# Order of loads and reuse of tiles in a one-core trunk of two gated linear-attention branches

## The chip, the cores and the metric

The kernel runs on one core of a Trainium2 chip. It uses five engines, which are called here as the profile names them: PE (TensorE, the matmuls, with PEld for its weight loads), DVE (VectorE), ACT (ScalarE), POOL (GpSimd) and SP (SyncE). Each engine works through its own instructions in order; DMA transfers are issued from the queue of one of them. The metric is the device time in microseconds (us) of the core, as the median of the runs. The kernel before took 1220.32 us (three runs, 1220.21 to 1222.69).

## The reference

The computation is one layer of a decoder trunk, batch 1, 1024 positions, width 1024, everything in float32:

```python
mod = silu(c) @ ada_w + ada_b
shift, scale, gate = split(mod, 3)
h = rms_norm(x, norm_w) * (1 + scale) + shift
hq, hf, hi, hz, gq, gk, gv, gz, ga, mg = split(h @ w_in)      # widths 4 x 1024, 2 x 512, 2 x 1024, 16, 2048
y_h = hgrn2_branch(hq, hf, hi, hz, lb, hgrn_norm_w)           # 8 heads of 128
y_g = gla_branch(gq, gk, gv, gz, ga, alpha_w, alpha_b, gla_norm_w)   # 4 heads, keys of 128, values of 256
u_h, u_g = y_h @ w_branch[0], y_g @ w_branch[1]
merged = sigmoid(mg[0]) * u_h + sigmoid(mg[1]) * u_g
out = rms_norm(x + gate * (merged @ w_out), final_norm_w)
```

Each branch is a causal gated recurrence, `S_t = diag(a_t) S_{t-1} + k_t v_t^T`, `o_t = S_t^T q_t`, computed in chunks of 64 positions, then normalised and multiplied by a SiLU gate.

## The kernel before

**Storage.** SBUF holds 46 slots of 128 x 1024 floats. `Slots.get` takes the slot that has been free longest (the free list is a plain queue), and names the tile by a serial number (`b_8146`), so that a high number is a late tile. `Halves` lends out halves of a slot. A new tile in a slot can be written only once every reader of the slot's last tile is done. Where that reader is a store to DRAM, the new tile's load or cast waits for the store.

**Products in three matmuls.** A float32 operand is parted into a high part, which ACT makes by a cast, and a low part, which DVE makes by a subtraction: `split` (cast L196, subtraction L197) in the first stages, `prep_duo` (L1333, L1334) and `build`, for the other operand (L1311, L1312, or L1308 with a sign, for one product of the seven), in the last. Each product is high by high, high by low, and low by high.

**First stages, to about 800 us.** `Stream` goes through jobs of the combined projection (matmuls L541, L352 and others), loading the weights of two jobs ahead and parting one ahead. Between its matmuls it weaves in two tracks, each a generator that yields a number of units of PE work after which it wants to go on:

- the side track: the projection's outputs through SiLU (for one, L952 and L953 read PE's bank), and the chunked attention (L657 to L850). Its solve of a block goes to and fro between engines: DVE L676 to L679, PE L683, DVE L687 to L710 with the masked copies L698, PE L715, and so on to DVE L785 and ACT L790 to L796;
- the back track, here called background: `prepare`, `gate_side` (eight rows of `ada_w` summed into the output gate) and `out_weights`. `prepare` forms differences of the activations, and by `weight_sums` (L1188 to L1209, additions around L1200) the sums of weight blocks that a Winograd form needs, and stores them to `ws`. `out_weights` loads `w_out` (`load_wy`), multiplies it by the gate (`gate_wy`, L1233), adds (`sum_wy`, L1242), and stores to `wo` from L1228.

**Last stages, from about 800 us.** Four blocks (two halves of `mg`, two branch projections) are each computed by seven products in a Winograd form. Each product takes two duos of weight tiles: 56 duos, each used by 24 matmuls at L1391. A duo is loaded by `load_duo` (L1322 whole from `ws`, or two halves by L1326 from `w_in` or `w_branch`), and parted by `prep_duo`. `ahead(n, loads, preps)` stands in front of duo n's matmuls and sees to it that all duos below n + loads have their load issued and all below n + preps are parted. `scale_quad` (L1290) multiplies the other operand by its normalisation for the last block. The results pass through ACT's copies (L1363, L1365, L1371) and DVE's sums (L1378); for the first block `put_gate1` takes a sigmoid (L1462) and stores it from POOL (L1463, `gate`), for the third DVE multiplies (L1477). Products by `w_out` and the final norm follow from L1537 on.

**What sets the order.** The program is emitted in the order of the code, with yields deciding where the tracks come in. The framework then puts each engine's instructions in order by its own estimates and by the dependencies, and adds the waits. So a change of the numbers in a yield, of the arguments of `ahead`, or of the slot that `get` returns may change the order on any engine. Loads are issued from SP, stores from POOL; within each queue they go in order.

Of the kernel before, what the change touches and what calls it, by code (L numbers as in the profile page):

```python
# [34 lines left out]
class Slots:  # L35


    def __init__(self, pool, n):
        self.pool = pool
        self.free_list = deque(range(n))  # L40
        self.owner = {}
        self.serial = 0

    def get(self, shape, dtype=F32):
        i = self.free_list.popleft()
        self.serial += 1
        t = self.pool.tile([P] + list(shape), dtype, tag=f"s{i}", name=f"b{self.serial}")
        self.owner[id(t)] = (i, t)
        return t

    def free(self, *tiles):
        for t in tiles:
            self.free_list.append(self.owner.pop(id(t))[0])


class Halves:
# [5 lines left out]
    def get(self):  # L62
        if not self.open:
            t = self.slots.get([2, 512])
            left = [0, t]
# [6 lines left out]
    def free(self, *views):  # L72
        for v in views:
            v, left = self.owner.pop(id(v))
            left[0] -= 1
            if left[0]:
                self.open.append((v, left))
            else:
                self.open = deque(z for z in self.open if z[1] is not left)
                self.slots.free(left[1])  # L80
# [3 lines left out]
def hybrid_trunk_kernel(  # L84
# [6 lines left out]
    nc = tc.nc  # L91
# [952 lines left out]
    def gate_side():  # L1044
# [3 lines left out]
        for k in range(KT):  # L1048
# [7 lines left out]
            yield 1  # L1056
# [102 lines left out]
    def factors(acts, f):  # L1159
        sub = nc.vector.tensor_sub  # L1160
        for kk in range(2):
# [7 lines left out]
            for p, dst, a, b in ((5, "11", "12", "11"), (7, "12", "12", "22"), (6, "22", "22", "11"), (4, "21", "21", "22")):  # L1169
                sub(y[dst], y[a], y[b])  # L1170
                nc.gpsimd.dma_start(f[p][kk], y[dst])
                if p == 7:
                    S.free(y["12"])
                elif p == 6:
                    S.free(y["11"])
                yield 1.5
            S.free(y["22"], y["21"])
# [10 lines left out]
    def weight_sums(b, i):  # L1188
# [19 lines left out]
        S.free(x1, x2, s1, s2)  # L1208
# [36 lines left out]
    def out_weights():  # L1245
        for kk in range(2):
            while len(S.free_list) < 12:
                yield 1
            load_wy(kk)
            yield 8  # L1250
# [7 lines left out]
            S.free(*wy.values())  # L1258
# [201 lines left out]
    def put_gate1(d, half, ap, summed):  # L1460
# [3 lines left out]
        Q.free(g)  # L1464
# [222 lines left out]
    def begin_2():  # L1687
        build(GROUPS[0])
        fetch_factor(GROUPS[1])
        ahead(0, 4, 1)  # L1690
# [38 lines left out]
```

## Time and profile before

| | kernel before |
|---|---|
| median of three runs | 1220.32 us |
| the profiled execution | 1226.09 us |
| span in its trace | 1224.2 us |
| granted TensorE clock, mean | 0.993 |
| busy PE / PEld | 1186.9 / 987.0 us |
| busy DVE / ACT / POOL | 793.4 / 548.5 / 124.4 us |
| read from HBM / written | 132.87 / 49.28 MB |
| mean transfer rate | 149 GB/s |

The span runs from the first to the last instruction in the trace; the execution's own time has a little around it. PE and PEld overlap. A row of the timeline gives a start, a duration, the engine, the line, output and inputs without their numbers, and in brackets the time that the engine was idle ahead of it and what ended the idle time. Line numbers in rows are those of the kernel that the row comes from.

### The profile page before, as it was taken

What the parts mean: (1) busy time and instruction counts of PE and PEld (TensorE: products, weight loads), DVE (VectorE), ACT (ScalarE), POOL (GpSimd) and SP (SyncE); (2) the same over time, 40 slices, a digit from 0 to 9 for tenths busy, and PEclk for the clock granted to TensorE, in tenths of its full rate; (3) what the DMA queues carried; (4) which work ended last, traced back from release to release, by engine and by line L of the source; (5) the groups of instructions that cost most, each with busy time, mean ns of one, the idle gap of its engine ahead of it and who ended that gap; (6) DMA issues with size and microseconds to landing.
All of it is one profiled execution on the core that took longest, in us unless ns stands there. A gap on an engine that the chain in (4) does not pass through costs nothing.

```text
span 1224.2 us, 20849 instructions
## 1 busy us (share of the span) xinstructions
PE 1186.9 (97%) x8575; PEld 987.0 (81%) x8575; DVE 793.4 (65%) x1247; ACT 548.5 (45%) x798; POOL 124.4 (10%) x215
## 2 busy tenths in 40 slices
PE   5999999999999999999999989999999999999997
PEld 3777889899898888888888878877778888878886
DVE  4636444774938465877787575694532666988994
ACT  5646722434344243424433324445733544544554
POOL 4100000202112122022011201011010000000000
PEclk9999999999999999999999999989999999999999
DMA  9714000845453267265165522144465646435523
GB/s 321 271 69 138 18 19 20 291 139 182 146 173 122 82 214 233 93 198 175 60 241 190 193 101 87 35 157 159 135 206 167 196 137 211 150 103 172 165 104 128
DMA packets 130960, 183.51 MB, mean 150 GB/s; under 512 B 7467, under 2 KB 97633, under 8 KB 130866
## 3 DMA queue, kind: packets, MB, share of 16 engines
q1 hardware_dynamic: 117250, 136.87, 36.1%
q0 software_dynamic: 13568, 45.31, 9.6%
q8 instruction: 67, 1.10, 0.4%
q14 instruction: 27, 0.22, 0.1%
q10 hardware_dynamic: 48, 0.01, 0.0%
HBM read 132.87 MB, written 49.28 MB: 149 GB/s over the span
## 4 chain that ended last, share of the span: by engine, by line
PE 59%; issue 22%; DMA 4%; ACT 3%; DVE 3%; POOL 2%; SPq 0%; POOLq 0%; ACTq 0%; DVEq 0%
PE pd L541 16%; PE pd L1391 10%; PE sc_ps L1391 5%; PE pm L1391 5%; PE pd L1537 3%; PE pd L643 2%; PE pd L644 2%; PE pd L645 2%; DMA b<-in_w_in_dram 2%; PE sc_ps L1537 2%; PE pm L848 1%; PE pm L829 1%; PE pm L850 1%; PE pd L352 1%; PE pm L1537 1%
## 5 line engine op out<-in xcount | busy, mean ns | idle before, releaser
L541 PE MATMUL pd<-b,b 128*128 128x512 f32 x1632 | 388.9, 395 | 0.0
L541 PEld LDWEIGHTS pd<-b,b 128*128 128x128 f32 x1632 | 303.3, 188 | 65.6 <-issue 1.7
L1391 PE MATMUL pd<-b,b 128*128 128x512 f32 x720 | 177.6, 399 | 8.6 <-ACT b L1462 3.0
L1391 PEld LDWEIGHTS pd<-b,b 128*128 128x128 f32 x720 | 136.9, 192 | 40.9 <-ACT b L1462 4.0
L197 DVE TENSOR_TENSOR b<-b,b 128x1024 fp32r<-128x1024 f32 (+2 forms) x90 | 99.2, 1114 | 79.0 <-ACT b L196 66.2
L196 ACT CAST b<-b 128x1024 fp32r<-128x1024 f32 (+2 forms) x90 | 84.0, 949 | 111.0 <-PE pd L541 19.9
L1334 DVE TENSOR_TENSOR b<-b,b 128x1024 fp32r<-128x1024 f32 x56 | 69.8, 1249 | 72.8 <-ACT b L1333 43.0
L1333 ACT CAST b<-b 128x1024 fp32r<-128x1024 f32 x56 | 58.3, 1048 | 65.2 <-PE pd L1391 18.9
L1391 PE MATMUL sc_ps<-b,b 128*128 128x512 f32 x324 | 79.4, 391 | 1.0 <-ACT scT L793 1.0
L600 PE MATMUL pd<-b,b 128*128 128x256 f32 x256 | 74.2, 290 | 0.0
L602 PE MATMUL pd<-b,b 128*128 128x256 f32 x256 | 72.5, 283 | 0.0
L601 PE MATMUL pd<-b,b 128*128 128x256 f32 x256 | 72.4, 283 | 0.0
L1391 PE MATMUL pm<-b,b 128*128 128x512 f32 x300 | 72.2, 389 | 0.0
L1391 PEld LDWEIGHTS sc_ps<-b,b 128*128 128x128 f32 x324 | 60.3, 188 | 14.3 <-ACT scT L793 1.4
L1312 DVE TENSOR_TENSOR b<-b,b 128x1024 fp32r<-128x1024 f32 x48 | 57.7, 1223 | 19.7 <-ACT b L1311 12.5
L1311 ACT CAST b<-b 128x1024 fp32r<-128x1024 f32 x48 | 49.7, 1048 | 44.7 <-PE pd L1391 15.8
L1391 PEld LDWEIGHTS pm<-b,b 128*128 128x128 f32 x300 | 56.5, 188 | 11.8
L352 PE MATMUL pd<-b,b 128*128 128x512 f32 x192 | 53.2, 410 | 1.6 <-ACT b L196 0.9
L1206 POOL DMA_DIRECT2D ws<-b x64 | 34.6, 541 | 192.0 <-DVE b L1200 86.5
L735 ACT COPY xb<-b 128x512 f32<-128x512 f32 x48 | 29.3, 620 | 52.5 <-PE sc_ps L715 23.6
L643 PE MATMUL pd<-b,b 128*128 128x512 f32 x128 | 51.2, 400 | 0.0
L644 PE MATMUL pd<-b,b 128*128 128x512 f32 x128 | 50.0, 390 | 0.0
(286 smaller groups left out, 1965.4 us busy)
## 6 DMA issues: line engine op xcount, KB each, us to landing
b<-in_w_in_dram SPq DMA_DIRECT2D x66, 512.0 KB, 4.4
ws<-b POOLq DMA_DIRECT2D x64, 256.0 KB, 3.2
b<-ws SPq DMA_DIRECT2D x32, 512.0 KB, 3.8
b<-in_x_dram SPq DMA_DIRECT2D x16, 512.0 KB, 6.0
b<-in_ada_w_dram SPq DMA_DIRECT2D x32, 256.0 KB, 6.7
b<-in_w_branch_dram SPq DMA_DIRECT2D x16, 512.0 KB, 4.5
b<-h SPq DMA_DIRECT2D x14, 512.0 KB, 4.6
wo<-b POOLq DMA_DIRECT2D x14, 512.0 KB, 3.8
```

Source lines behind the costliest of these rows:

```text
L196: nc.scalar.copy(hi, src)
L197: nc.vector.tensor_sub(lo, src, hi.bitcast(F32))
L352: nc.tensor.matmul(accs[f], wg(a, d, f), b[d][:, half * 512:half * 512 + 512], start=(d == 0 and n == 0), stop=(d == KT - 1 and n == 2))
L541: nc.tensor.matmul(ps[0:w, th * 512:(th + 1) * 512], a[:, k, 0:w], b[:, th * 512:(th + 1) * 512], start=(k == 0 and n == 0), stop=(k == KT ...
L600: nc.tensor.matmul(o, lh, hi[:, k % 4, :], start=(k == 0), stop=False)
L601: nc.tensor.matmul(o, lh, lo[:, k % 4, :], start=False, stop=False)
L602: nc.tensor.matmul(o, ll, hi[:, k % 4, :], start=False, stop=(k == KT - 1))
L643: nc.tensor.matmul(o, lh, hi[:, k % 2, :], start=(k == 0), stop=False)
L644: nc.tensor.matmul(o, lh, lo[:, k % 2, :], start=False, stop=False)
L1334: nc.vector.tensor_sub(lo, t, hi.bitcast(F32))
L1391: nc.tensor.matmul(o, a[:, sl], c, start=(p in (1, 5) and kt == 0 and n == 0), stop=(kt == 3 and n == 2), skip_group_check=True)
L1537: nc.tensor.matmul(o, a, b, start=(p in (1, 5) and kt == 0 and n == 0), stop=(kt == 3 and n == 2), skip_group_check=True)
```

## The change

Three things change; no computation is added or taken away.

**The free list** becomes a heap. A freed slot gets as its key the serial number of the latest tile taken so far, and `get` returns the lowest key. A slot that is freed behind a store (`sent=True`: the activations in `put_act`, the differences and sums in `prepare`, the `w_out` tiles, the gate halves in `put_gate1`) gets a key that is eight higher, as if it had been freed eight tiles later.

**The background.** `gate_side` yields 1.5 units after each row in place of 1. `load_wy` loads one tile in a call, and `out_weights` yields 2 units after each of the four and 2 more behind them, where before all four loads stood together, with 8 units behind them.

**The last stages.** `ahead` is called with 5 and 1 in place of 4 and 2 (in `begin_2`, ahead of the first duo, 5 and 1 in place of 4 and 1): a duo's load is issued one duo earlier, and its cast and subtraction come one duo later.

```diff
 class Slots:
-        self.free_list = deque(range(n))
+        self.free_list = [(-1, i - n, i) for i in range(n)]
+        self.freed = 0
 ...
     def get(self, shape, dtype=F32):
-        i = self.free_list.popleft()
+        i = heapq.heappop(self.free_list)[-1]
 ...
-    def free(self, *tiles):
+    def free(self, *tiles, sent=False):
         for t in tiles:
-            self.free_list.append(self.owner.pop(id(t))[0])
+            self.freed += 1
+            heapq.heappush(self.free_list, (self.serial + (8 if sent else 0), self.freed, self.owner.pop(id(t))[0]))
 ...
     # Halves.free
+            left[2] |= sent
             if left[0]:
                 self.open.append((v, left))
             else:
                 self.open = deque(z for z in self.open if z[1] is not left)
-                self.slots.free(left[1])
+                self.slots.free(left[1], sent=left[2])
 ...
     def put_act(acts, d, y):
-        S.free(y)
+        S.free(y, sent=True)
 ...
     # gate_side, after each row
             S.free(b)
-            yield 1
+            yield 1.5
 ...
     # factors (and so the two frees ahead of it)
-            S.free(y["22"], y["21"])
+            S.free(y["22"], y["21"], sent=True)
 ...
     # weight_sums
-        S.free(x1, x2, s1, s2)
+        S.free(x1, x2)
+        S.free(s1, s2, sent=True)
 ...
-    def load_wy(kk):
-        for kh in range(2):
-            for f in range(2):
-                t = wy[kh, f] = S.get([2, 512])
-                nc.sync.dma_start(t, w_rows[kh][:, 2 * kk:2 * kk + 2, f * 512:f * 512 + 512])
+    def load_wy(kk, n):
+        kh, f = n // 2, n % 2
+        t = wy[kh, f] = S.get([2, 512])
+        nc.sync.dma_start(t, w_rows[kh][:, 2 * kk:2 * kk + 2, f * 512:f * 512 + 512])
 ...
     # out_weights
-            load_wy(kk)
-            yield 8
+            for n in range(4):
+                load_wy(kk, n)
+                yield 2
+            yield 2
 ...
-            S.free(*wy.values())
+            S.free(*wy.values(), sent=True)
 ...
     # last_stages
-                    ahead(2 * n + i // 2, 4, 2)
+                    ahead(2 * n + i // 2, 5, 1)
 ...
     # put_gate1
-        Q.free(g)
+        Q.free(g, sent=True)
 ...
     # begin_2
-        ahead(0, 4, 1)
+        ahead(0, 5, 1)
```

The changed file has four lines more ahead of `out_weights` and six more ahead of the last stages: L197 there is L201, L679 is L683, L698 is L702, L1233 is L1237, L1242 is L1246, L1334 is L1340, L1462 is L1468.

At three places the rows of an engine are shown, first of the kernel before and then of the changed one. The first is DVE at the solve of an attention block, some 710 us into the span of the kernel before. `xb` is the solve's operand, on which PE's matmul L683 (L687 in the changed kernel) waits; the rows on 128x1024 tiles are subtractions of weights and products of the background.

```order
769 L676 TENSOR_TENSOR xb<-b_6490,b_6552 128x32x8
770 L677 TENSOR_TENSOR xb<-b_6490,b_6552 128x32x8x2
771 L685 TENSOR_TENSOR b_6490<-b_6490,b_6552 128x256
772 L678 TENSOR_TENSOR xb<-xb,b_6552 128x32x16
773 L197 TENSOR_TENSOR b_7015<-b_6864,b_7014 128x1024
774 L679 TENSOR_TENSOR xb<-xb,b_6552 128x32x8
775 L687 TENSOR_TENSOR b_6552<-b_6552 128x256
```

The same place of DVE in the changed kernel:

```order
768 L682 TENSOR_TENSOR xb<-xb,b_6550 128x32x16
769 L1237 TENSOR_TENSOR b_6871<-b_6871,b_6058 128x1024
770 L683 TENSOR_TENSOR xb<-xb,b_6550 128x32x8
771 L691 TENSOR_TENSOR b_6550<-b_6550 128x256
772 L690 TENSOR_TENSOR b_6488<-xb,b_6550 128x256x3
773 L692 TENSOR_TENSOR b_6550<-b_6550 128x256
774 L201 TENSOR_TENSOR b_7015<-b_6862,b_7014 128x1024
775 L705 TENSOR_TENSOR tot_726<-b_6550 128x256
776 L1246 TENSOR_TENSOR b_6767<-b_6767,b_6871 128x1024
777 L694 TENSOR_TENSOR blk<-sc_ps,eye_679 128x256
```

The weight subtraction has moved from ahead of the last `xb` row to four rows behind it, and two background rows on `w_out` tiles (L1237 and L1246) have come in, one ahead of that row.

The second is ACT in the first of the last stages, some 900 us into the span. The casts L1333 (L1339) make the high parts of duos; the L1462 (L1468) on `pd` frees the bank for which PE's next matmuls wait.

```order
492 L1333 CAST b_8261<-b_8191 128x1024
493 L1462 ACTIVATE b_7872<-b_7872 128x512
494 L1462 ACTIVATE b_7938<-b_7938 128x512
495 L1333 CAST b_8331<-b_8265 128x1024
496 L1333 CAST b_8298<-b_8228 128x1024
497 L1462 ACTIVATE b_7938<-b_7938 128x512
498 L1462 ACTIVATE b_8243<-pd_7492 128x512
```

The same place of ACT in the changed kernel:

```order
493 L1468 ACTIVATE b_7870<-b_7870 128x512
494 L1468 ACTIVATE b_7936<-b_7936 128x512
495 L1339 CAST b_8297<-b_8145 128x1024
496 L1468 ACTIVATE b_7936<-b_7936 128x512
497 L1339 CAST b_8394<-b_8264 128x1024
498 L1468 ACTIVATE b_8242<-pd_7494 128x512
499 L1339 CAST b_8361<-b_8227 128x1024
```

Of the two casts that stood together ahead of the last two sigmoids, b_8298 (now b_8297) stands one sigmoid earlier, and b_8331 is no longer there: in front of the sigmoid on `pd` stands the cast of another tile (b_8394), and the loads' tiles have lower numbers.

The third is DVE at about 1035 us, where it makes the low parts of duos for PE's next products.

```order
1014 L1290 TENSOR_TENSOR b_9157<-b_9157,b_7956 128x1024
1015 L1378 TENSOR_TENSOR b_9129<-b_9129,sc_ps 128x512
1016 L1290 TENSOR_TENSOR b_9158<-b_9158,b_7956 128x1024
1017 L1477 TENSOR_TENSOR b_8751<-b_8751,b_9129 128x512
1018 L1334 TENSOR_TENSOR b_9162<-b_9081,b_9161 128x1024
```

The same place of DVE in the changed kernel:

```order
1014 L1296 TENSOR_TENSOR b_9156<-b_9156,b_7954 128x1024
1015 L1384 TENSOR_TENSOR b_9128<-b_9128,sc_ps 128x512
1016 L1296 TENSOR_TENSOR b_9157<-b_9157,b_7954 128x1024
1017 L1483 TENSOR_TENSOR b_8750<-b_8750,b_9128 128x512
1018 L1340 TENSOR_TENSOR b_9161<-b_9002,b_9160 128x1024
```

The rows stand in the same order, but the subtraction in the last of them reads another load (b_9002 in place of b_9081): it belongs to the duo one before.

More of the change, by code (lines that the diff above doesn't have):

```diff
@@ L1 @@
+import heapq
 from collections import deque
@@ L64, in get @@
             t = self.slots.get([2, 512])
-            left = [0, t]
+            left = [0, t, False]
             self.open.extend((t[:, i, :], left) for i in range(2))
@@ L70, in get, with free @@
         return v
-    def free(self, *views):
+    def free(self, *views, sent=False):
         for v in views:
@@ L1172, in factors @@
                 if p == 7:
-                    S.free(y["12"])
+                    S.free(y["12"], sent=True)
                 elif p == 6:
-                    S.free(y["11"])
+                    S.free(y["11"], sent=True)
                 yield 1.5
-            S.free(y["22"], y["21"])
+            S.free(y["22"], y["21"], sent=True)
     def branch(n, d):
```

## The prediction

> **What bounds the kernel now.** I read, in this order, the page's busy times, the busy time by stretches of the span, the TensorE timeline where a stretch loses time, and the chain that ended last. Line numbers are those of the kernel before.
>
> ```profile
> PE 1186.9 (97%) x8575; PEld 987.0 (81%) x8575; DVE 793.4 (65%) x1247; ACT 548.5 (45%) x798; POOL 124.4 (10%) x215
> ```
>
> TensorE (PE) is busy 97% of the span, so only what makes PE wait, or run slowly, counts. By stretches (span, then busy us of PE, PEld, DVE, ACT, POOL, then granted clock, DMA share, GB/s):
>
> ```profile
> 700.00:750.00 50.00, 46.85 (x438) 38.50 (x437) 31.70 (x59) 16.89 (x27) 1.59 (x3) 0.97 0.30 95
> 800.00:850.00 50.00, 45.66 (x422) 36.23 (x421) 34.14 (x59) 25.27 (x41) 5.22 (x6) 0.93 0.46 155
> 850.00:900.00 50.00, 46.45 (x212) 37.65 (x210) 24.92 (x24) 32.00 (x40) 7.22 (x10) 1.00 0.56 176
> 900.00:950.00 50.00, 48.76 (x208) 40.17 (x209) 12.17 (x10) 18.58 (x27) 2.69 (x5) 0.97 0.55 176
> 1032.00:1080.00 48.00, 48.00 (x212) 39.35 (x211) 46.14 (x51) 21.83 (x25) 0.00 (x0) 1.00 0.50 152
> ```
>
> The first four lose 3.15, 4.34, 3.55 and 1.24 us. The last loses nothing on PE, but there DVE is busy 46.14 of 48. The PE timeline shows where the loss sits (start, us, what, and in brackets the wait before it and its releaser):
>
> ```profile
> 717.35 1.76 PE L683 MATMUL sc_ps<-xb,b 128*32 128x80 f32 x64 [3.15 <-DVE xb L679]
> 719.04 6.89 PE L541 MATMUL pd<-b,b 128*128 128x512 f32 x24
> 725.85 0.89 PE L715 MATMUL sc_ps<-xb,b 128*32 128x48 f32 x64
> ...
> 814.59 8.49 PE L1391 MATMUL pd<-b,b 128*128 128x512 f32 x24 [2.96 <-DVE b L953]
> 823.01 0.89 PE L715 MATMUL sc_ps<-xb,b 128*32 128x48 f32 x64
> ...
> 839.49 1.88 PE L1391 MATMUL sc_ps<-b,b 128*128 128x512 f32 x7 [0.97 <-ACT scT L793]
> 841.66 1.19 PE L1391 MATMUL pd<-b,b 128*128 128x512 f32 x4 [0.29 <-ACT b L1462]
> ...
> 857.92 3.02 PE L1391 MATMUL pd<-b,b 128*128 128x512 f32 x12 [1.17 <-ACT b L1363]
> ...
> 887.38 3.02 PE L1391 MATMUL pd<-b,b 128*128 128x512 f32 x12 [0.94 <-DVE b L1378]
> ...
> 894.77 2.88 PE L1391 MATMUL pd<-b,b 128*128 128x512 f32 x12
> 897.49 1.07 PE L1391 MATMUL pm<-b,b 128*128 128x512 f32 x4
> 901.24 4.58 PE L1391 MATMUL pd<-b,b 128*128 128x512 f32 x12 [2.68 <-ACT b L1462]
> 905.62 4.80 PE L1391 MATMUL pm<-b,b 128*128 128x512 f32 x20
> ...
> 1087.93 1.21 PE L1391 MATMUL pd<-b,b 128*128 128x512 f32 x4 [0.44 <-DVE b L1483]
> ```
>
> I call the three large ones A (717), B (814) and C (901). Start to start, 12 matmuls take 2.72 us from 894.77 to 897.49, so 24 take 5.44. After A they take 6.81 (719.04 to 725.85), after B 8.42 (814.59 to 823.01), and after C 12 take 4.38 (901.24 to 905.62): PE runs slowly behind each large wait, for 1.37, 2.98 and 1.66 us more. Waits (12.60) and slowness (6.01) are 18.6 us together, 1.5% of the time: the most that better ordered loads could give.
>
> The Trainium skill, page "TensorE: Matmul & The Clock Gate", section "Part 1: The HAM clock gate", says that the clock halves after at least one idle window of some 3.4 us. Here it fell behind waits of 2.68 and 2.96 us, so the trace disagrees on the bound. By the Trainium skill a shorter wait costs itself alone; what that would make of the sum is a rival below.
>
> The chain names what was late:
>
> ```profile
> 702.54 3.27 DMA wo<-b
> 706.30 7.96 DMA b<-in_w_in_dram
> ...
> 886.29 3.86 DMA gate<-b
> 891.79 6.30 DMA b<-in_w_in_dram
> ```
>
> Ahead of A and of C stands the same pair: a store (wo, gate), and then a load into the tile or through the queue that the store held up. This is what the change works on.
>
> **The change, place by place.** The heap and the yields run while the program is built and cost the chip nothing. No load, store, cast or subtraction is added or taken away; all are moved, in the order of each engine and of SP's queue. So each term is a wait that goes or comes. The profiled execution took 1226.09 us (span 1224.2 and 1.89 around it), 5.77 above the median of 1220.32; I work out waits in it and take their sum from the median.
>
> A. DVE works in order, and L679, which PE awaits, stands behind a weight subtraction L197:
>
> ```profile
> 711.01 0.88 DVE L678 TENSOR_TENSOR xb<-xb,b 128x512 f32<-128x512 f32 x1
> 715.43 1.23 DVE L197 TENSOR_TENSOR b<-b,b 128x1024 fp32r<-128x1024 f32 x1 [3.53 <-ACT b L196]
> 716.57 0.63 DVE L679 TENSOR_TENSOR xb<-xb,b 128x256 f32<-128x256 f32 x1
> ...
> 723.77 0.43 DVE L698 COPY_PREDICATED blk<-mask,sc_ps 128x64 f32<-128x64 int32 x1
> ```
>
> In the changed order L197 stands four rows later, and ahead of L679 comes a gate product L1233, whose load goes out beside the same w_in load at about 706 (both tiles are freed by PE's L541). Nothing shows how long that load takes there: between the page's median for such loads (4.4, below) and the 7.96 above it lands at 710.4 to 714.0. With 1.23 for L1233 and 0.63 for L679, behind L678's end at 711.9, L679 ends between 713.8 and 715.9; PE is free at 714.2 (717.35 less 3.15). I take no wait, since two wo stores that run at that time before are now queued later; 1.7 is the other end. But from L679 to L698 DVE now carries L197 and one L1242 more (1.2 each) and one L717 (0.9) less: 7.6 us (716.57 to 724.20) become 9.1. From 713.2 that ends at 722.3, and PE reaches L715 at 714.2+1.7+5.44 = 721.3. What is late next is L698, by 1.0. A gives 3.15+1.37-1.0 = 3.5; its ends are 0.5 and 4.5.
>
> ```profile
> b<-in_w_in_dram SPq DMA_DIRECT2D x66, 512.0 KB, 4.4
> ```
>
> B. ScalarE (ACT) holds the release of PE's bank (L952, then DVE's L953) behind a cast whose target waits for a store:
>
> ```profile
> 808.83 2.00 ACT L1311 CAST b<-b 128x1024 fp32r<-128x1024 f32 x2 [4.23 <-DMA yh<-b]
> 810.73 1.06 ACT L1308 ACTIVATE b<-b 128x1024 fp32r<-128x1024 f32 x1
> 811.69 1.00 ACT L952 ACTIVATE b<-pd 128x1024 f32<-128x1024 f32 x1
> ```
>
> The changed order still has a cast that waits for this yh store (an L1333 now): all other tiles are in use, so ranking the tile later only names another user. L1308 moves behind L952, but three DVE subtractions stay ahead of L953. B gives 0.4, between -0.5 (the store 0.9 later) and 1.0 (the L1308).
>
> 838 to 842. L1308 (1.06) no longer stands ahead of the sigmoid L1462, and one cast has left ACT's row there; DVE's last step of the block solve (L785) follows some 0.6 sooner. Of 0.97 and 0.29 I take 0.9; ends 0 and 1.3. At 887 the subtraction L1334 moves behind L1378, for which PE waits 0.94: 0.8, ends 0 and 0.94. 857 stays: it hangs on GpSimd's L1110, which does not move.
>
> C. SP issues in order, and its queue is held by the gate stores:
>
> ```profile
> 879.81 12.48 SPq L1326 DMA_DIRECT2D b<-in_w_in_dram  x8
> ...
> 898.18 1.99 ACT L1333 CAST b<-b 128x1024 fp32r<-128x1024 f32 x2 [4.58 <-DMA b<-in_w_in_dram]
> 900.08 0.62 ACT L1462 ACTIVATE b<-b 128x512 f32<-128x512 f32 x1
> 900.61 0.58 ACT L1462 ACTIVATE b<-pd 128x512 f32<-128x512 f32 x1
> ```
>
> Eight half loads take from 879.81 to 892.3; the last pair lands at 898.1 (891.79 + 6.30); two casts wait for it and PE's L1462 stands behind them. With tiles behind gate stores ranked later, three of these four duos wait for matmuls or subtractions that end between 861 and 866, and go out then, some 14 to 25 us sooner. Of ACT's two casts one moves behind the L1462 and the other waits only for PE at 894. The L1462 comes at 896.8+0.6+0.6 = 898.0 (PE itself 0.9 earlier), where PE is free at 897.7. C gives 2.68+1.66, less 0.3: 4.0; ends 1.0 (the wait halves, the clock still falls) and 4.3. At 1087 an L1334 leaves DVE ahead of L1483: 0.4, ends 0 and 0.44.
>
> New waits. Parting one duo later takes 5.44 us, one step's matmuls, from every duo's lead. Compared with their first use, most leads stay above 3 us. In the stretch with DVE busy 96% one does not:
>
> ```profile
> 1036.15 1.23 DVE L1334 TENSOR_TENSOR b<-b,b 128x1024 fp32r<-128x1024 f32 x1
> ```
>
> The L1334 at 1036.15 belonged to the duo that PE takes at 1041.3; in that place now stands the duo that PE needs at 1036.3. It ends at 1037.4: a wait of 1.1. It gives the following duos 1.1 more, and with DVE's durations laid end to end they then come 0.4 to 2 us in time. The unseen cost reaches from 0.5 to a whole step, 5.4. At 824 an L1308 now stands ahead of PE's L1365: 0.4, ends 0 and 1. At 497 an L1200 that waits for a load and a store stands where L197 stood ahead of L679:
>
> ```profile
> 495.01 1.22 DVE L197 TENSOR_TENSOR b<-b,b 128x1024 fp32r<-128x1024 f32 x1
> 496.14 0.63 DVE L679 TENSOR_TENSOR xb<-xb,b 128x256 f32<-128x256 f32 x1
> 497.35 1.31 PE L683 MATMUL sc_ps<-xb,b 128*32 128x80 f32 x64
> ```
>
> Its load can go out at about 490.7, when the last reader of its tile ends, so by 4.4 to 7.96 it lands at 495.1 to 498.7; L1200 and L679 add 1.3: 0 to 2.6 late, and I take 0.5. The gate rows and the w_out loads, spread over more steps, end well before their L1233; I cost that at nothing, covered by 4 us or more of PE work ahead of their use.
>
> Sum: 3.5+0.4+0.9+0.8+4.0+0.4 = 10.0 gained, 1.1+0.4+0.5 = 2.0 lost, so 8.0, and 1212.3. The profiled run is slow by 5.77 for reasons unseen; if part of its stalls is missing in timed runs, so is part of the gain, and I forecast 1213.
>
> **Rivals.** *A background load holds DVE in order* (slower). For it: the load before A took 7.96, not 4.4, and the changed order has such a row directly ahead of L679 at 497, 542 and 714. Against: by the issues worked out above only the slow price makes them late. Each such wait costs what A cost, 3.15+1.37 = 4.5. If 714 waits as before, its 3.5 is gone; with 4.5 at 497 and 542 too, against 0.5, the sum is 8.0-3.5-8.5 = -4.0: 1224.3. It decides from the third such place on; with two it is no change. The Trainium skill, "DMA: Bandwidth & Descriptors", section "Issuing engines are not separate DMA queues", says that loads and stores of all issuers share 16 engines; the 7.96 beside wo stores agrees, and speaks against loads that go out earlier in a bunch.
>
> *Half the gain*: one of A and C keeps its wait since the next late item is as late (a wo store for L1242, a gate store for the other cast). For it: B, where the changed order keeps the store. 8.0 less 3.5 or 4.0: about 1216.
>
> *Slow PE has another cause* and stays behind A and C: 8.0-1.37-1.66 = 5.0, 1215.3. Against it: 24 matmuls are slow behind A, B and C only. (The Trainium skill's 3.4 us would leave the same.)
>
> *Nothing moves that counts*: tiles are so scarce that the heap returns the same waits, as at B: 1220. Against: at C the predecessors differ.
>
> *B goes too*: 2.96+2.98 more, 1207.
>
> **How the numbers follow.** Forecast 0.44 (1209 to 1215); half the gain 0.15; slow PE 0.05; B too 0.03: faster together 0.67. Nothing 0.08. Slower 0.25. A measurement of this kernel tells some 0.2% (2.4 us) from no change. The range from 1207 to 1224.5 takes in the slower case at its price and leaves out the part of it that costs more.
>
> **What would show it.** Right: no PE wait over 0.5 at L683 near 714, one near 1 at L715; none over 0.5 at L1462 near 898, and its 12 matmuls in 2.72; B as before; one of about 1 near 1028 at L1391, released by L1334. Wrong: waits at L683 near 497 or 542 released by L679; PE waiting for L1334 in step after step from 1030 to 1080; w_in loads over 6 us at C.

## The result, and the profile after

The changed kernel takes 1232.61 us (median of five runs, 1230.35 to 1233.43) against 1221.18 us for the kernel before (five runs). The ratio is 1.0087, with a 95% interval from 1.0070 to 1.0104: it is slower, and lies outside the range that was forecast. The profiled execution took 1233.43 us (span 1231.7).

The page of the changed kernel gives nearly the same busy times as before, in 7.5 us more of span:

```profile
PE 1188.9 (97%) x8575; PEld 986.9 (80%) x8575; DVE 795.5 (65%) x1247; ACT 548.2 (45%) x798; POOL 122.7 (10%) x215
```

The busy time of the changed kernel by stretches (columns as in the prediction):

```profile
200.00:250.00 50.00, 45.64 (x396) 40.86 (x396) 26.32 (x38) 15.90 (x19) 8.01 (x12) 0.96 0.60 214
350.00:400.00 50.00, 46.16 (x399) 41.15 (x398) 29.59 (x53) 21.63 (x26) 9.39 (x14) 0.97 0.53 174
710.00:760.00 50.00, 49.29 (x455) 40.65 (x454) 35.87 (x63) 16.14 (x27) 3.20 (x6) 1.00 0.33 117
800.00:850.00 50.00, 45.92 (x432) 36.77 (x431) 40.25 (x65) 26.33 (x40) 4.52 (x5) 0.97 0.46 156
850.00:900.00 50.00, 48.54 (x233) 39.88 (x233) 25.52 (x29) 33.22 (x45) 7.23 (x10) 1.00 0.59 186
900.00:950.00 50.00, 50.00 (x221) 41.13 (x221) 13.99 (x13) 21.22 (x29) 3.79 (x7) 1.00 0.57 190
```

The stretches of A and C, from 700 to 750 and from 850 to 950, have mostly recovered, and 800 to 850 (B) has not, as forecast. But two stretches in which PE was busy for 50.00 of 50 us before, from 200 to 250 and from 350 to 400, now lose 4.36 and 3.84 us, with a lower granted clock. The timeline of PE in the changed kernel shows what they are, and what became of A, B and the place at 1036:

```profile
235.73 7.09 PE L545 MATMUL pd<-b,b 128*128 128x512 f32 x30
247.19 1.51 PE L719 MATMUL sc_ps<-xb,b 128*32 128x48 f32 x64 [4.36 <-DVE tot L722]
...
392.07 0.89 PE L719 MATMUL sc_ps<-xb,b 128*32 128x48 f32 x64 [3.84 <-DVE tot L722]
...
735.87 0.89 PE L719 MATMUL sc_ps<-xb,b 128*32 128x48 f32 x64 [0.71 <-DVE blk L702]
...
825.18 7.37 PE L1397 MATMUL pd<-b,b 128*128 128x512 f32 x24 [3.66 <-DVE b L957]
...
1041.29 2.58 PE L1397 MATMUL pd<-b,b 128*128 128x512 f32 x10 [1.23 <-DVE b L1340]
...
1047.33 2.60 PE L1397 MATMUL pd<-b,b 128*128 128x512 f32 x10 [0.28 <-DVE b L1340]
```

Both new waits stand at the second matmul of an attention block's solve (L719, which was L715). In the kernel before PE came to it without a wait. Its rows there, and those of DVE that lead to it, in the second trace of the kernel before (the first experiment below):

```profile
242.43 0.89 PE L715 MATMUL sc_ps<-xb,b 128*32 128x48 f32 x64
...
380.58 0.89 PE L715 MATMUL sc_ps<-xb,b 128*32 128x48 f32 x64
```

```profile
236.53 0.68 DVE L710 TENSOR_TENSOR xb<-b,tot 128x512 f32<-128x512 f32 x1
...
240.53 0.38 DVE L718 TENSOR_TENSOR tot<-tot 128x64 f32<-128x64 f32 x1
240.71 1.25 DVE L197 TENSOR_TENSOR b<-b,b 128x1024 fp32r<-128x1024 f32 x1
...
373.96 1.23 DVE L197 TENSOR_TENSOR b<-b,b 128x1024 fp32r<-128x1024 f32 x1 [1.06 <-DMA ws<-b]
375.11 0.68 DVE L710 TENSOR_TENSOR xb<-b,tot 128x512 f32<-128x512 f32 x1
```

L710 begins the part of the solve on DVE that the matmul waits for, and L718 ends it 4.4 us later (236.53 to 240.91). So it was done 1.5 us before PE needed it near 247, and near 392, where a subtraction already stood ahead of L710 and waited 1.06 us for a `ws` store, 1.1 us before (375.11 and 4.38 more, against 380.58). DVE and ACT of the changed kernel show what was late. Near 247, ACT's cast waits for a `yg` store, with the solve's copy L712 behind it, and DVE's L1174 for a load of `h`:

```profile
238.53 1.05 ACT L200 CAST b<-b 128x1024 fp32r<-128x1024 f32 x1 [3.88 <-DMA yg<-b]
239.49 0.40 ACT L712 COPY xb<-b 128x256 f32<-128x256 f32 x1
```

```profile
239.96 1.23 DVE L201 TENSOR_TENSOR b<-b,b 128x1024 fp32r<-128x1024 f32 x1 [6.86 <-ACT xb L712]
241.66 1.22 DVE L1174 TENSOR_TENSOR b<-b,b 128x1024 f32<-128x1024 f32 x1 [0.48 <-DMA b<-h]
242.80 0.68 DVE L714 TENSOR_TENSOR xb<-b,tot 128x512 f32<-128x512 f32 x1
...
381.94 0.69 DVE L1204 TENSOR_TENSOR b<-b 128x512 f32<-128x512 f32 x1 [5.97 <-DMA yg<-b]
...
387.08 0.69 DVE L1205 TENSOR_TENSOR b<-b,b 128x512 f32<-128x512 f32 x1 [2.52 <-DMA ws<-b]
387.69 0.69 DVE L714 TENSOR_TENSOR xb<-b,tot 128x512 f32<-128x512 f32 x1
```

Near 392, background additions wait for a `yg` and a `ws` store. L714 (L710 before) stands behind all of these in DVE's order, and near 247 behind an L201 and an L1174 that came after it before. From L714 to the end of L722 (L718 before), for which PE waits, it is 4.4 us as before (242.80 to 247.16), so PE gets what is late in full.

Where the time went can be read place by place, since the two traces hold the same 8575 matmuls in nearly the same order: the start of the n-th matmul after, less its start before, is the delay so far, and the table gives how much it grows in each stretch. The kernel before was traced twice (the second is the first experiment below), and the changed kernel is compared with both.

| stretch of before, us | forecast | against first trace | against second |
|---|---|---|---|
| 0 to 240 | 0 | -0.8 | +0.3 |
| 240 to 260 | 0 | +7.2 | +7.0 |
| 260 to 380 | 0 | +0.1 | +0.3 |
| 380 to 400 | 0 | +5.5 | +5.5 |
| 400 to 500 (497) | +0.5 | +1.2 | +1.2 |
| 500 to 600 | 0 | +1.2 | +1.2 |
| 600 to 700 | 0 | -0.4 | -0.3 |
| 700 to 720 (A) | -3.5 | -4.1 | -5.0 |
| 720 to 800 | 0 | -0.1 | +0.3 |
| 800 to 860 (B, 824, 838) | -0.9 | -0.8 | +0.2 |
| 860 to 940 (887, C) | -4.8 | -5.5 | -3.0 |
| 1020 to 1060 (1036) | +1.1 | +2.2 | +2.2 |
| 1060 to 1200 (1087) | -0.4 | +1.4 | +1.3 |
| sum | -8.0 | +7.1 | +11.3 |

Stretches that are not listed differ by less than 0.05 us. The last column agrees with the medians (11.4).

### The profile page after: what moved, and what is told of

It is laid out like the page before. It is cut to its first block, busy times and chain, and to the rows that moved or that the text cites. A ratio compares the mean times of both kernels' runs of the same rounds, so it can differ in the third digit from the quotient of the medians.

```text
span 1231.7 us, 20853 instructions
## 1 busy us (share of the span) xinstructions
PE 1188.9 (97%) x8575; PEld 986.9 (80%) x8575; DVE 795.5 (65%) x1247; ACT 548.2 (45%) x798; POOL 122.7 (10%) x215
## 4 chain that ended last, share of the span: by engine, by line
PE 67%; issue 15%; DVE 5%; DMA 3%; POOL 3%; ACT 2%; POOLq 0%; ACTq 0%; DVEq 0%
PE pd L545 19%; PE pd L1397 12%; PE sc_ps L1397 6%; PE pm L1397 5%; PE pd L1543 3%; PE pd L606 2%; PE pd L605 2%; PE pd L604 2%; POOL ws L1210 2%; PE pm L852 2%; PE sc_ps L1543 2%; PE pm L854 2%; PE pm L833 1%; PE pd L356 1%; PE pd L647 1%
## 5 line engine op out<-in xcount | busy, mean ns | idle before, releaser
L201 DVE TENSOR_TENSOR b<-b,b 128x1024 fp32r<-128x1024 f32 (+2 forms) x90 | 100.8, 1130 | 70.8 <-ACT b L200 55.0
L1340 DVE TENSOR_TENSOR b<-b,b 128x1024 fp32r<-128x1024 f32 x56 | 69.6, 1249 | 62.7 <-ACT b L1339 42.3
L1339 ACT CAST b<-b 128x1024 fp32r<-128x1024 f32 x56 | 58.5, 1050 | 53.8 <-PE pd L1397 16.8
```

The costliest lines, as they stand in the source:

```text
L201: nc.vector.tensor_sub(lo, src, hi.bitcast(F32))
L1340: nc.vector.tensor_sub(lo, t, hi.bitcast(F32))
```

## The experiments

An edit is shown as a diff against the kernel named ahead of it. The ranked free list without any mark (`sent=True`) is the plain queue of before, so that the marks are what it changes.

**The kernel before, traced again.** No edit.

> The kernel before, unchanged, for a second trace. Against the first trace of before, the changed kernel's trace ends only 7.2 us later (1223.37 against 1216.22 for the last matmul), while the medians differ by 11.4. If the first trace held some 4 to 5 us of stalls that its other executions do not have, the new trace is shorter by about that, and the row shows at which of the places 717, 814, 887 or 901 (waits of 3.15, 2.96, 0.94 and 2.68 us) it was. If the difference lies outside the trace, all four waits come back as they were. Median 1221, within 0.2% of the kernel before either way.

Measured: 1221.42 us, ratio 1.0004 (0.9987 to 1.0020). The last matmul starts at 1212.1 in place of 1216.2 in the first trace. The wait at 901 is 1.83 where it was 2.68; the waits A and B are there as before, but behind B and C the clock no longer falls. PE in the second trace:

```profile
716.40 1.76 PE L683 MATMUL sc_ps<-xb,b 128*32 128x80 f32 x64 [3.41 <-DVE xb L679]
...
813.98 2.32 PE L1391 MATMUL pd<-b,b 128*128 128x512 f32 x8 [3.05 <-DVE b L953]
```

The busy time with the granted clock (the number behind POOL's) in the stretches behind A, B and C, first trace:

```profile
718.10:721.50 3.40, 3.40 (x40) 2.69 (x30) 3.26 (x6) 0.93 (x2) 0.00 (x0) 0.50 0.00 0
813.60:820.50 6.90, 5.91 (x14) 4.67 (x15) 6.90 (x13) 2.29 (x5) 0.00 (x0) 0.51 0.24 76
902.40:905.80 3.40, 3.40 (x10) 2.63 (x9) 1.23 (x1) 0.00 (x0) 0.00 (x0) 0.50 0.66 198
```

and second trace:

```profile
717.10:720.50 3.40, 3.40 (x42) 2.69 (x32) 3.26 (x6) 0.93 (x2) 0.00 (x0) 0.50 0.00 0
814.00:817.40 3.40, 3.40 (x14) 2.55 (x15) 3.40 (x7) 1.29 (x2) 0.00 (x0) 1.00 0.05 12
898.70:902.10 3.40, 3.40 (x15) 2.82 (x16) 0.58 (x2) 0.38 (x1) 0.79 (x2) 1.00 0.46 163
```

So the first expectation holds in the main: the first trace has 13.7 us at half clock where the second has 3.4, and its mean granted clock, 0.993, equals the lowest of the 21 executions of the kernel before that were run beside this one (0.993 to 0.999). Half of the 10.3 between the traces is 5.2 us, and they differ by 4.1. By places these are 1.3 in the first 50 us, which have nothing to do with A to C, 1.0 from 800 to 860 and 2.5 at 860 to 940, less 0.7 elsewhere. Behind B the full clock gains 2.4 us up to 820, but PE then waits 1.4 more at later matmuls, so a stretch at half clock need not cost half its length.

**The ranking undone**, in the changed kernel:

```diff
-        i = heapq.heappop(self.free_list)[-1]
+        i = self.free_list.popleft()
 ...
-            heapq.heappush(self.free_list, (self.serial + (8 if sent else 0), ...))
+            self.free_list.append(self.owner.pop(id(t))[0])
```

> The changed kernel with the plain free list back; the yields and the calls of ahead stay changed. Theory (the ranking of tiles behind a store makes the new waits): the two waits of PE at L719 (4.36 and 3.84 us near 247 and 392) are gone and with them 12.7 us; the wait of 2.7 us at 901 is back; the gain at 717 (4.1) stays and the loss from 1036 to 1120 (some 3.5) too: about 1220. Rival (the yields or the later parting make the new waits): both waits at L719 stay, about 1233.

Measured: 1221.98 us, ratio 0.9999 (0.9983 to 1.0014). PE's waits for the solve's second matmul shrink to two small ones (total, times, longest):

```profile
PE sc_ps L715 <- DVE tot L718: 1.2, 2, 0.6
```

The theory holds for them: without the ranking nothing is lost near 247 and 392. The sum has other parts than expected, though. Against the second trace of before it loses 4.1 near 678, where nothing stood in the changed kernel, and 2.1 between 720 and 800; it gains 5.0 at 717, 3.0 at 800 to 860 and 2.7 at 901, where the wait was expected back; and it loses 3.1 behind 1020. ACT and PE near 678 show a weight cast that waits for its load, with the solve's copies behind it:

```profile
673.51 1.05 ACT L196 CAST b<-b 128x1024 fp32r<-128x1024 f32 x1 [7.15 <-DMA b<-in_w_in_dram]
674.46 1.06 ACT L790 COPY scT<-sc_ps 32x128 f32<-32x128 f32 x4
```

```profile
678.48 3.30 PE L829 MATMUL pm<-b,b 128*128 128x128 f32 x14 [2.42 <-ACT b L808]
```

**The ranking alone**, in the kernel before: the heap and all its marks.

```diff
-        i = self.free_list.popleft()
+        i = heapq.heappop(self.free_list)[-1]
 ...
-        S.free(y)
+        S.free(y, sent=True)
 ...
-            S.free(y["22"], y["21"])
+            S.free(y["22"], y["21"], sent=True)
 ...
-        S.free(x1, x2, s1, s2)
+        S.free(x1, x2)
+        S.free(s1, s2, sent=True)
 ...
-            S.free(*wy.values())
+            S.free(*wy.values(), sent=True)
 ...
-        Q.free(g)
+        Q.free(g, sent=True)
```

> The kernel before with the ranked free list alone; yields and ahead as before. Theory (the ranking makes the new waits): +7.2 near 247 and +5.5 near 392, about +2.3 between 490 and 580, and -5.5 at 887 to 901, with 717 as before: about 1230. Rival (yields or ahead make them): only the gain at 901, about 1215.

Measured: 1232.65 us, ratio 1.0089 (1.0060 to 1.0118), as slow as the whole change. PE:

```profile
247.64 1.51 PE L719 MATMUL sc_ps<-xb,b 128*32 128x48 f32 x64 [4.11 <-DVE tot L722]
...
391.25 0.89 PE L719 MATMUL sc_ps<-xb,b 128*32 128x48 f32 x64 [2.72 <-DVE tot L722]
```

Both waits are there: +6.7 and +3.6, and +3.3 from 480 to 600, +1.4 from 600 to 660. At 717, which was expected as before, 4.0 us are gained.

**Late marks only**, in the changed kernel: the marks on `w_out` tiles and gate halves stay.

```diff
-        S.free(y, sent=True)              # put_act
+        S.free(y)
 ...
-            S.free(y["22"], y["21"], sent=True)   # factors, and the two ahead of it
+            S.free(y["22"], y["21"])
 ...
-        S.free(s1, s2, sent=True)         # weight_sums
+        S.free(s1, s2)
```

> The changed kernel in which only the w_out tiles and the gate halves are ranked behind a store; the tiles of put_act, of factors and of weight_sums are freed as in the kernel before. Theory (the two waits near 247 and 392 come from those early marks alone): both are gone, the gains at 717 (4.1), 887 to 901 (5.5) and 814 (0.8) stay, the loss of 3.5 behind 1036 stays: about 1214. Rival (any ranking, or the other parts, makes the waits): they stay, about 1232. Second rival (the waits were a coincidence of times that another place repeats): one of them comes back elsewhere, about 1219.

Measured: 1228.20 us, ratio 1.0061 (1.0038 to 1.0084); its traced execution was the quickest of six (1224.45). The early waits are gone (-0.2 and 0.0), so they come from the early marks; but 2.5 us near 678, 2.0 from 720 to 800, 1.3 from 800 to 860 and 3.1 behind 1020 are lost, and 1214 is far. The second rival, that a wait comes back elsewhere, fits best, and the place is that of the run before.

**put_act's mark taken out**, in the changed kernel:

```diff
-        S.free(y, sent=True)              # put_act
+        S.free(y)
```

> The changed kernel with one mark taken out: the activations that put_act stores (yg, yh) are freed as in the kernel before; the marks in factors, weight_sums, on the w_out tiles and the gate halves stay. Theory (the two waits near 247 and 392 come from put_act's mark, since the cast ahead of the first and the addition ahead of the second wait for a yg store): both are gone, and the kernel does as with late marks alone, about 1227. Rival (the marks in factors or weight_sums make them): they stay, 1232 or more.

Measured: 1237.87 us, ratio 1.0137 (1.0109 to 1.0166), the slowest of all. No wait is left at the two matmuls (+1.5, which stands at a later matmul of the solve, L774, and 0.0), which is what the theory said of them. Its time is 11 us off the forecast. The two other early marks, those in `factors` and `weight_sums`, are what it has more than the kernel with late marks only, which shows no loss at 497; here DVE and PE show an addition behind a `ws` store ahead of the solve's first matmul:

```profile
499.95 0.69 DVE L1204 TENSOR_TENSOR b<-b 128x512 f32<-128x512 f32 x1 [5.64 <-DMA ws<-b]
```

```profile
506.09 2.36 PE L687 MATMUL sc_ps<-xb,b 128*32 128x80 f32 x64 [5.13 <-DVE xb L683]
```

It costs 7.7 us there; 2.3 are lost from 260 to 380, and 2.7 near 678.

**Late marks in the kernel before**: the heap, and of its marks only two:

```diff
-            S.free(*wy.values())
+            S.free(*wy.values(), sent=True)
 ...
-        Q.free(g)
+        Q.free(g, sent=True)
```

> The kernel before with the ranked free list and only the marks on the w_out tiles and the gate halves; yields and ahead as before. Theory (each part brings its own new wait, and the late marks none): the wait at 901 falls (3 us or more), 717 and the order up to 700 are as before, there is no wait near 678 and no loss behind 1036: about 1218. Rival (ranking is what makes the runs of the late-marks kernel slow): 1225 or more.

Measured: 1214.41 us, ratio 0.9937 (0.9922 to 0.9952): faster than both kernels. Against the second trace of before: -5.0 at 717, -1.4 from 800 to 860, -2.5 at 860 to 940, and nothing lost behind the first 50 us. That 717 goes was not expected, since DVE's order there is that of before. DVE, first in the second trace of before and then in this kernel:

```profile
714.48 1.23 DVE L197 TENSOR_TENSOR b<-b,b 128x1024 fp32r<-128x1024 f32 x1 [3.79 <-ACT b L196]
```

```profile
712.11 1.23 DVE L201 TENSOR_TENSOR b<-b,b 128x1024 fp32r<-128x1024 f32 x1 [0.16 <-ACT b L200]
```

The same subtraction stands ahead of the same step of the solve, and is no longer late.

**ahead at 5 and 1 alone**, in the kernel before:

```diff
-                    ahead(2 * n + i // 2, 4, 2)
+                    ahead(2 * n + i // 2, 5, 1)
 ...
-        ahead(0, 4, 1)
+        ahead(0, 5, 1)
```

> The kernel before with ahead at 5 and 1 alone. Theory (parting one duo later costs at 1036 and behind it what the traces with ahead at 5 and 1 lose there): +3 from 1020 to 1120 in the trace, nothing before 800, something between -3 and +3 at 814 to 900: about 1225. Rival (the loss there needs the other parts): no loss from 1020 to 1120, 1222.

Measured: 1219.51 us, ratio 0.9985 (0.9972 to 0.9997). The loss of 3.1 from 1020 on is there, so it belongs to this part; but 1.3 at 800 to 860 and 2.6 at 860 to 940 are gained, so that the whole comes out level, not slower. PE (the L1334 for which it waits is the parting of a duo):

```profile
1029.78 2.60 PE L1391 MATMUL pd<-b,b 128*128 128x512 f32 x10 [0.91 <-DVE b L1334]
...
1035.84 2.56 PE L1391 MATMUL pd<-b,b 128*128 128x512 f32 x10 [0.28 <-DVE b L1334]
```

**The background's spacing alone**, in the kernel before:

```diff
-            yield 1
+            yield 1.5
 ...
-            load_wy(kk)
-            yield 8
+            for n in range(4):
+                load_wy(kk, n)
+                yield 2
+            yield 2
```

> The kernel before with the yields and the parted w_out loads alone. Theory (they move a weight cast ahead of the block solve's copies near 670, and take the subtraction away at 717): +2.4 to +4.1 near 678 with a wait at L829 for L808, -4 to -5 at 717, +1.4 near 775: about 1222. Rival (the wait near 678 needs the ranked tiles or ahead): no wait there, about 1218.

Measured: 1225.38 us, ratio 1.0026 (1.0011 to 1.0040). The wait near 678 is there (+2.3), 717 is gained (-5.0), 1.9 are lost from 720 to 800. In this trace 2.3 us are also lost at 860 to 940, where the clock falls behind C as in the first trace of before, and 2.4 near 392, behind a wait of 2.32 at L715, though the order on PE, DVE, ACT and POOL is that of before up to 600; in the other two runs with the spacing and without early marks there is none. DVE shows that it is the store wait that stood there in the kernel before (1.06 us), only longer:

```profile
378.34 1.23 DVE L197 TENSOR_TENSOR b<-b,b 128x1024 fp32r<-128x1024 f32 x1 [2.18 <-DMA ws<-b]
379.49 0.69 DVE L710 TENSOR_TENSOR xb<-b,tot 128x512 f32<-128x512 f32 x1
```

So that place is near its limit in the kernel before too.

**put_act's mark alone**, in the kernel before: the heap, and of its marks only one:

```diff
-        S.free(y)                         # put_act
+        S.free(y, sent=True)
```

> The kernel before with the ranked free list and put_act's mark alone. Theory (this mark makes the waits of PE at the solve's second matmul near 247 and 392): both are there, together 10 to 13 us, and 717 and 901 stay as before: 1231 to 1234. Rival (they need the marks of factors and weight_sums as well): neither is there, 1222.

Measured: 1230.94 us, ratio 1.0060 (1.0040 to 1.0081). Half of the theory falls: 2.5 us near 247, with a wait of 2.33, and nothing at 392. The time is near the forecast for other reasons: against the second trace of before 717 costs 1.5 more, 800 to 860 costs 1.1 more, and 860 to 940 costs 2.2 more.

**put_act's and factors' marks**, and **put_act's and weight_sums' marks**, each in the kernel before with the heap. The second mark of the first and of the second:

```diff
-            S.free(y["22"], y["21"])      # factors, and the two ahead of it
+            S.free(y["22"], y["21"], sent=True)
```

```diff
-        S.free(x1, x2, s1, s2)            # weight_sums
+        S.free(x1, x2)
+        S.free(s1, s2, sent=True)
```

> The kernel before with the ranked free list and the marks of put_act and of factors. put_act's mark alone gave 2.5 us near 247 and nothing at 392, all marks gave 7 and 3.7 to 5.5. Theory (the rest near 247 comes from factors' mark, which puts the cast that follows a yg store ahead of a load that is late too): 7 us near 247; what is missing at 392 comes from the mark in weight_sums, whose addition follows a ws store: nothing there. With -0 elsewhere about 1231. Rival (any two early marks make both): 7 near 247 and 4 or more at 392, 1233 or more.

> The kernel before with the ranked free list and the marks of put_act and of weight_sums. Theory: 2.5 us near 247 as with put_act's mark alone, and 3.7 to 5.5 at 392 with a wait of the addition for a ws store: about 1231. Rival (392 needs all three early marks): 2.5 near 247, nothing at 392, as put_act's mark alone.

Measured: 1234.93 us (ratio 1.0102, 1.0087 to 1.0117) and 1234.82 us (1.0103, 1.0086 to 1.0119). At the two places both give what the theory says: with `factors` +6.6 near 247 and nothing at 392, with `weight_sums` +2.4 and +5.1. So the full loss near 247 needs the marks of `put_act` and `factors`, and the one at 392 those of `put_act` and `weight_sums`. The reason given for `factors` is not borne out: ACT's casts there stand in the same order with and without it, and only the wait for the `yg` store grows (2.13 us with `put_act`'s mark alone, 3.52 with both). The times are 4 us longer than forecast, by other places: 1.3 and 2.9 from 400 to 600, 1.4 and 0.8 from 260 to 380, 2.1 and 0.9 at 717. PE with the marks of `put_act` and `factors`:

```profile
247.25 1.51 PE L719 MATMUL sc_ps<-xb,b 128*32 128x48 f32 x64 [4.50 <-DVE tot L722]
```

DVE with those of `put_act` and `weight_sums`:

```profile
378.06 0.69 DVE L1204 TENSOR_TENSOR b<-b 128x512 f32<-128x512 f32 x1 [5.69 <-DMA yg<-b]
...
383.37 0.69 DVE L1205 TENSOR_TENSOR b<-b,b 128x512 f32<-128x512 f32 x1 [2.68 <-DMA ws<-b]
```

**The w_out mark alone**, and **the gate mark alone**, in the kernel before with the heap (one each of the two hunks of the late marks above):

> The kernel before with the ranked free list and the mark on the w_out tiles alone. With both late marks the wait at 717 went (5 us) although DVE's order there is that of before. Theory (the weight load that was late there no longer waits for a wo store, which is the mark's doing): -5 at 717, the wait at 901 as before, about 1217. Rival (717 went through the gate halves' mark or by luck): 717 as before, 1221.

> The kernel before with the ranked free list and the mark on the gate halves alone. Theory (this mark alone takes away the waits at 887 to 901): -2.7 or more there, 717 as before, about 1218. Rival (the gain there needs the w_out mark): 1221.

Measured: 1215.59 us (ratio 0.9935, 0.9915 to 0.9955) and 1217.16 us (0.9955, 0.9933 to 0.9978). The `w_out` mark shrinks the wait at 717 to 0.41 (-4.5 with the half clock), and the gate mark takes 1.9 at 860 to 940. What held SP's queue ahead of the load at 717 (L523, L527 in the changed file) can be read for 690 to 716, first in the second trace of before and then with the `w_out` mark (total, times, longest):

```profile
SPq L1278 <- DMA wo<-b: 12.3, 2, 7.5
```

```profile
SPq L527 <- PE pd L545: 6.7, 1, 6.7
```

Before, a load of `h` (L1278) in front of it waits for a `wo` store, as the prediction's chain had it; with the mark alone the weight load waits for PE only. It also takes less time, 6.0 us from its issue to the cast in place of 7.4. With the gate mark the wait at 717 stays (3.03 us), but the half clock behind it does not come, which gives 1.8. The `w_out` mark's trace also has 1.6 us more at 240 to 260, where its order is that of before: the place near 247 is near its limit too.

**Late marks with ahead at 5 and 2**, against late marks in the kernel before:

```diff
-                    ahead(2 * n + i // 2, 4, 2)
+                    ahead(2 * n + i // 2, 5, 2)
 ...
-        ahead(0, 4, 1)
+        ahead(0, 5, 1)
```

> The kernel with the two late marks and ahead at 5 and 2: loads five duos ahead, parted two ahead as before. Theory (what costs 3 us from 1020 to 1120 is the later parting, not the earlier load): no loss there; at 901 ACT's order has a cast of a load ahead of the sigmoid again, so that some of the gain there may go: 1213 to 1217. Rival (the earlier loads cost, by crowding SyncE's queue): a loss of 2 or more behind 1020, 1217 or more. Second rival (the earlier loads pay by themselves): 1211.

Measured: 1218.10 us, ratio 0.9957 (0.9941 to 0.9973). Nothing is lost behind 1020: the later parting is what costs there, and not the earlier load. But the wait at B grows to 3.69, and 3.7 us are lost from 800 to 860, a place that no expectation named; at 860 to 940 the gain is 1.8.

## Why the prediction was wrong

**The sum.** It forecast -8.0, and the second trace gives +11.3. Of the 19.3 us between, 12.5 are the two waits near 247 and 392 (8.2 of waiting, 4.3 of half clock behind them). The rest is small: +1.5 better at 717, and worse by 1.1 at 800 to 860, 1.8 at 860 to 940, 1.9 from 400 to 600, 2.8 behind 1020, and 0.6 elsewhere (12.5 - 1.5 + 1.1 + 1.8 + 1.9 + 2.8 + 0.6 = 19.2, with rounding).

**The step that failed** is the list of new waits. It priced places where a changed row stands ahead of L679, the first matmul's operand in a solve (497, 542, 714), and the parting of duos. It followed the solve to its second matmul only at A. Elsewhere it left out the rows ahead of L710, with which that matmul's part of the solve begins, and so the solves near 247 and 392, where 1.5 and 1.1 us were to spare and the ranking puts a store-bound cast and store-bound additions. So the sum held no price for the early marks ahead of 497. Without the ranking both losses are gone, with the ranking alone both are there, and the one at 392 is not there where the mark of `put_act` or that of `weight_sums` is left out.

**The slower rival** named the mechanism, background work that holds DVE in order ahead of a solve, with a chance of 0.25. It erred in the place (247 and 392 for 497 and 542), in the kind (mostly tiles that follow a store, where the rival spoke of loads), and in the price: 7.0 and 5.5 in place of 4.5, since the waits were longer (4.36 and 3.84 for 3.15) and the half clock behind them took more (2.6 and 1.7 for 1.37). Its "third such place" was not needed.

**A** was right in size: 3.5 forecast, 4.1 to 5.0 measured, with 0.71 at the solve's next matmul where 1.0 was said to be left. Its reason was half right. The change takes L197 out of DVE's way, but the mark on `w_out` tiles alone takes the wait away with L197 still there.

**B** was right in kind: an L1339 still waits for the `yh` store there. The wait is 3.66 (2.96 and 3.05 before), longer than the worst end allowed, and where 0.9 was to be gained from 800 to 860, 0.2 is lost against the second trace.

**C** was right in kind, and no w_in load or L1462 holds PE there any more. Its size hung on the execution: -5.5 against the first trace, -3.0 against the second. Against the second trace the gate mark alone gives 1.9 and `ahead` alone 2.6, so that the two together hardly give more than one.

**1036** was right in kind and place (wait 1.23 for L1340, 1.1 forecast), but the sentence that the following duos come in time was wrong: 0.28 more is waited at the next step, and with what follows up to 1120 the later parting costs 3.1 to 3.5 where 0.7 was allowed (1.1 at 1036 less 0.4 at 1087).

**497** was within its ends (+1.2; 0 to 2.6). At 542, which the sum held at nothing, PE waits 0.75 behind an addition that waits for a load. That the spaced w_out loads cost nothing was wrong wherever `put_act`'s mark is absent: with them 2.3 to 4.1 are lost near 678.

**"The most that better ordered loads could give"**, 18.6 us, was read from an execution with 13.7 us at half clock. The prediction noted that this execution was slow by 5.77 for reasons unseen. Of these, 4.1 are missing in the second trace, most of them at places where the clock did not fall again; 1.3 of them, at the start, are something else.

What stays open is how the framework's estimates came to put each background row where it stands: the runs show which mark moves which wait, not why the estimate takes the row for early. Nor do they show why the spaced loads and `ahead` at 5 and 1, together with the late marks, lose 10 us against the late marks alone (late marks only against late marks in the kernel before): 2.5 of it near 678, 2.5 from 720 to 800, 2.8 from 800 to 860 and 3.1 behind 1020 are located, and explained only in part.

## What to carry to other kernels

When a change reranks buffers for a whole program, price it at every place where a latency chain goes to and fro between engines, and at each link of the chain: here one unlisted link, twice, cost more than all the gains. Test such a rule by region, because its parts don't add: two different edits, the spacing and the `w_out` mark, each removed the same wait at 717, and the marks that pay (after 700 us, 0.6% faster alone) were hidden by those that cost (before 600). Give stalls read from one trace a second trace before they are counted as gains.

## What the runs showed of the hardware

PE's granted clock halves in whole steps: in the 16 traces every slow stretch between the start and the end lasts 3.4 or 6.8 us, at 0.50. Within a trace these stretches keep to one grid of 3.413 us: in the first trace they begin at 718.07, 813.64 and 902.39, which are 28.0 and 26.0 steps apart. What follows a wait is not fixed by its length, but by how the wait falls on this grid. In the late-marks version of the kernel before, a wait of 2.00 us (806.74 to 808.74) lies whole within the step that ends at 808.92, and one slow stretch follows:

```profile
808.90:812.30 3.40, 3.40 (x9) 2.66 (x10) 3.40 (x9) 1.08 (x2) 0.00 (x0) 0.50 0.44 130
```

With the gate mark alone a wait of 3.03 us up to 716.40 is followed by none. The next fall of its clock, at 1210.02, lies 145 steps behind 715.09, and that edge of the grid cuts the wait in two, so that PE is idle for 1.72 us in one step (3.41 less 1.69) and for 1.31 in the next:

```profile
711.68:715.09 3.41, 1.69 (x8) 1.07 (x6) 0.61 (x1) 1.04 (x1) 0.00 (x0) 1.00 0.64 199
715.09:718.51 3.42, 2.11 (x68) 1.89 (x69) 3.38 (x6) 0.76 (x2) 0.00 (x0) 1.00 0.02 7
```

Counted over the steps of all 16 traces between 25 and 1205 us, with PE's idle time as the rows give it: each of the 28 steps at full clock in which PE is idle for 1.80 us or more is followed by half clock, and of the 56 in which it is idle for 1.0 to 1.8 us one is (1.52 us, with `ahead` alone). Of the steps at half clock, those with 0.67 us idle or more are followed by another, those with 0.58 or less are not. The count was made on these traces alone, and no kernel was changed to try it.

So a wait of 2 to 3 us costs itself, or up to 1.7 us more, or up to 3.4 more, and which of them depends on where the grid lies in that execution. That fits the scatter of the kernel before (1216.88 to 1225.94 in 21 runs): the seven of these with a mean granted clock of 0.997 or more take 1220.1 us in the mean, the thirteen with 0.995 or less 1223.1. The Trainium skill, "TensorE: Matmul & The Clock Gate", section "Part 1: The HAM clock gate", tells of a free-running activity window of about 3.4 us, by whose phase the same kernel may run differently; the lengths and the grid here agree with that, while waits of 2.0 us that halve the clock are shorter than the idle window it asks for.
